# Mixer C's block merges in 64x64 corners, row broadcasts by one transpose, layer 0's modulation tiles in pairs, and eight more modulation sums beside the first FF matrix

## Chip, cores and metric

One Trainium2 chip, one of its cores. The metric is device time in microseconds from the start of the program to its end, as the median of several runs; a profiled execution of the same program gives the trace. TensorE's granted clock has two levels, 1.2 and 2.4 GHz, which the profile gives as 0.50 and 1.00.

## What is computed

Two layers of a backbone with three parallel token mixers and an MLP, for a stream of 128 context tokens and one of 256 latent tokens, all in fp32:

```python
# two layers (DEPTH = 2), residual stream x of 128 context and 256 latent tokens, D_MODEL = 1024, fp32
mod = silu(cond) @ w_ada[l] + b_ada[l]                       # 6 x 1024 per stream: shifts, gains, gates
sh1, sc1, g1, sh2, sc2, g2 = split(mod, 6)
h = rmsnorm(x, norm1_g) * (1 + sc1) + sh1
a, b, c, gates = split(h @ w_in)                              # one input projection, 6576 columns
oa = window_attention(a)                                      # mixer A, 8 heads, sink logits, cached context
ob = latent_attention(b)                                      # mixer B, 8 heads, compressed latents
oc = bidir_gated_delta(c)                                     # mixer C, 4 heads, two directions, chunks
y = sum_j sigmoid(gates_j) * (o_j @ w_branch[j])              # three merges
x = x + g1 * (y @ w_out)
h = rmsnorm(x, norm2_g) * (1 + sc2) + sh2
x = x + g2 * (square(relu(h @ w_ff1)) @ w_ff2)                # D_FF = 4096
# after both layers: final rmsnorm; also returned: keys, values, latents and the final states of C
# inside mixer C, per chunk:  t_mat = inverse(eye + a_mat), a_mat strictly lower triangular
```

## The kernel before

**Layout.** Hidden states stand as 8 tiles of 128 channels by T = 384 tokens. A projection (`project`, L504) takes one weight tile of 128x1024, split by `split` (L146) into two parts `hi` and `lo` on ScalarE and VectorE, and issues 3 x 8 matmuls of 384 columns on TensorE (`mm3`, L150 to L153), into one of three PSUM banks of the pool `pg`. Weights come by `weights` (L131) through three raw buffers `raw` of the pool `wp`, by DMAs on the queue of SyncE (SP). Other PSUM pools are `pc` (two banks, tag c, `bank()`), `pf` (one pair of banks, tag f, `twin()`) and `po` (one bank).

**What sets the order.** All loops are unrolled. A planner puts the instructions of each engine into one fixed order by priority, estimated time and due buffers; each engine then works through its own order and waits on semaphores. `phase` and `stream` (L67, L73) give the priorities: within a phase of a layer what stands in the stream "chain" goes first, "fill" after it. So TensorE's order is a chain (mixer C, then mixer B) with projections of the merges filled in where the planner expects the chain to wait. `tc.issue_after(i)` makes the matmuls traced inside it follow `i` in the order, so that a run of small matmuls stays together.

**Mixer C** (L786 to L973). Per chunk n of 128 tokens (three: one of context, two latent) and direction d (two), a unit triangular system of 128x128 per head (four heads) is inverted: VectorE solves the 32x32 diagonal blocks of all by substitution (L844 to L849), the results are turned (L851, L853), and a loop over n and d (L859 to L899) merges blocks of 32 into 64 and of 64 into 128. In it `bdmask` (L107) spreads the 32x32 results over the block diagonal (L870), `mask5` (L865) takes the blocks beside the diagonal, four products of 128x128x128 per step run over the heads (L876, L884), four of 64 columns (L881), and two steps of four 64x64x64 products (L891, L896) with copies between. f32 products are recorded as two matmuls each. Then the recurrence over chunks follows (`new_values`, `correct`, `write_state`, `outputs`; tiles `g`, 24 buffers), and mixer B in the next phase. `merge(0)` (mixer A's) fills around mixer C, `merge(2)` (C's) around mixer B, `merge(1)` (B's) comes last; a merge is eight blocks of a gate projection and half as many matmuls for the branch (L512 to L535).

**Row broadcasts.** `rstd_rows` (L200) and the end of mixer C (L983 to L986) need a value per token as a row on all partitions. `pieces` (L177) cuts the column into three bf16 parts with four small VectorE steps, `rows` (L188) multiplies each, broadcast, with a bf16 identity: three matmuls per column of 128 tokens. 24 columns per layer: 3 for each of four norms, 12 for mixer C.

**Modulation.** Layer 0's first third is made at the start (`lead`); `ada` (L277) makes the rest beside `merge(2)` and `merge(1)`: each step loads one tile of 128x1024 of `w_ada` (512 KB) and issues four products into four column strips, then yields; `merge` takes `steps` of them per block, (1, 1) beside `merge(2)` from the raw weight buffers, (3, 3) beside `merge(1)` from three buffers `araw`. For layer 1 `ada_sums` (L294) sums 96 tiles of 256 KB on VectorE (L313, two instructions a tile) during layer 0's FF, one tile per block of the first matrix (32 blocks, L1118) and two per quarter row of the second (L1140), and brings each quarter's sums through 8 small products into the strips (L319).

## Time and profile before

| | before |
|---|---|
| median of 3 runs | 1564.96 us (1561.77 to 1565.35) |
| profiled execution | 1564.52 us |
| its span, first to last instruction | 1562.7 us |
| mean granted clock | 0.993 |
| DMA over the span | 134 GB/s read and written, 0.43 of 16 engines |

The span is what the trace covers; the execution's own time has 1.8 us around it. In the rows below, PE is TensorE's matmul row and PEld its weight loads, DVE is VectorE, ACT is ScalarE. Matmuls are pipelined: a row's duration goes from issue to a modelled end, and the next one starts long before that end. L-numbers are lines of the kernel; out<-in gives the program's tile names, then partitions x columns.

### The profile page before, as it was taken

Reading aid. Unit: us, or ns where it says so; the run is one execution under the profiler, and the core shown is the slowest. Engines: PE = TensorE matmul, PEld = TensorE weight load, DVE = VectorE, ACT = ScalarE, POOL = GpSimd, SP = SyncE. Lnnn points to the kernel's source line nnn. Section 1 sums busy time; section 2 is a strip of 40 time slices with the busy share of each in tenths; the row PEclk is TensorE's granted clock in tenths of the full one; section 3 lists DMA queues with packets and bytes.
Section 4 is the critical chain, followed back from the end, with each engine's and each line's share of the span. In section 5 each row is a group of like instructions: output and inputs, shape, how many; then the busy total and the mean of one; then the engine's idle time right before and its main releaser. Section 6 shows DMA issues by size and latency. Waiting matters only on the chain.

```text
span 1562.7 us, 25131 instructions
## 1 busy us (share of the span) xinstructions
PE 1521.6 (97%) x9652; PEld 1396.2 (89%) x9652; DVE 1013.9 (65%) x2187; ACT 771.8 (49%) x1522; POOL 12.9 (1%) x34
## 2 busy tenths in 40 slices
PE   5999999999999999999999999999999999999998
PEld 3898788987888999999988987889888999999997
DVE  4667896475435877789986778955655565553332
ACT  3466633346524666643344676334465446664222
POOL 0000100000000000000000001000000000000000
PEclk9999999999999999999998999999999999999999
DMA  9532131143488555578763331311424434433332
GB/s 315 162 103 88 48 95 48 59 145 105 141 291 279 160 175 176 176 236 259 252 187 98 95 95 47 96 49 58 129 61 135 130 118 126 126 122 129 128 122 81
DMA packets 80857, 212.82 MB, mean 136 GB/s; under 512 B 8801, under 2 KB 24545, under 8 KB 80609
## 3 DMA queue, kind: packets, MB, share of 16 engines
q1 hardware_dynamic: 80736, 211.21, 42.7%
q8 instruction: 76, 1.25, 0.3%
q14 instruction: 45, 0.36, 0.1%
HBM read 204.59 MB, written 4.75 MB: 134 GB/s over the span
## 4 chain that ended last, share of the span: by engine, by line
PE 86%; DVE 8%; DMA 4%; ACT 1%; issue 1%; SPq 0%; DVEq 0%; ACTq 0%
PE g L151 22%; PE g L153 22%; PE g L152 22%; PE c L156 9%; PE f L156 3%; DMA araw<-in_w_ada_dram 2%; PE o L156 2%; PE f L443 2%; DVE wlo L148 2%; PE g L156 1%; DVE h L847 1%; DVE blk L849 1%; DMA mraw<-in_w_ada_dram 1%; PE c L151 1%; PE c L153 1%
## 5 line engine op out<-in xcount | busy, mean ns | idle before, releaser
L147 ACT CAST whi<-raw 128x1024 fp32r<-128x1024 f32 x268 | 280.8, 1048 | 463.6 <-PE g L152 408.0
L153 PE MATMUL g<-hh,wlo 128*128 128x384 f32 (+1 forms) x1440 | 495.2, 345 | 2.8 <-DVE wlo L148 2.7
L151 PE MATMUL g<-hh,whi 128*128 128x384 f32 (+1 forms) x1440 | 494.8, 345 | 3.1 <-ACT hh L229 1.5
L152 PE MATMUL g<-hl,whi 128*128 128x384 f32 (+1 forms) x1440 | 493.6, 344 | 1.3 <-DVE hl L230 1.0
L148 DVE TENSOR_TENSOR wlo<-raw,whi 128x1024 fp32r<-128x1024 f32 x268 | 326.0, 1217 | 168.5 <-PE g L153 123.1
L151 PEld LDWEIGHTS g<-hh,whi 128*128 128x128 f32 x1440 | 272.2, 189 | 14.9 <-issue 6.3
L153 PEld LDWEIGHTS g<-hh,wlo 128*128 128x128 f32 x1440 | 272.5, 189 | 12.4 <-DVE wlo L148 6.0
L152 PEld LDWEIGHTS g<-hl,whi 128*128 128x128 f32 x1440 | 272.2, 189 | 8.1 <-issue 2.7
L151 PE MATMUL g<-fh,whi 128*128 128x384 f32 x512 | 172.9, 338 | 0.0
L152 PE MATMUL g<-fl,whi 128*128 128x384 f32 x512 | 172.1, 336 | 0.0
L153 PE MATMUL g<-fh,wlo 128*128 128x384 f32 x512 | 172.1, 336 | 0.0
L313 DVE SCALAR_TENSOR_TENSOR aacc<-araw,cs,aacc 128x512 f32<-128x512 f32 x168 | 116.5, 747 | 11.0 <-DMA araw<-in_w_ada_dram 6.9
L151 PEld LDWEIGHTS g<-fh,whi 128*128 128x128 f32 x512 | 96.2, 188 | 1.6 <-issue 1.6
L152 PEld LDWEIGHTS g<-fl,whi 128*128 128x128 f32 x512 | 96.3, 188 | 0.0
L153 PEld LDWEIGHTS g<-fh,wlo 128*128 128x128 f32 x512 | 96.3, 188 | 0.0
L156 PE MATMUL c<-g,g 128*128 128x128 f32 (+1 forms) x608 | 77.5, 274 | 3.6 <-DVE g L870 3.1
L156 PEld LDWEIGHTS c<-g,g 128*128 128x128 f32 (+1 forms) x608 | 69.9, 182 | 11.3 <-ACT g L878 4.0
L151 PE MATMUL g<-brh,whi 128*128 128x384 f32 x192 | 66.4, 346 | 0.4 <-ACT whi L147 0.4
L152 PE MATMUL g<-brl,whi 128*128 128x384 f32 x192 | 65.7, 342 | 0.0
L153 PE MATMUL g<-brh,wlo 128*128 128x384 f32 x192 | 65.6, 342 | 0.0
L424 ACT ACTIVATE at_p<-at_p,at_nm 128x384 f32<-128x384 f32 (+1 forms) x96 | 51.8, 541 | 24.7 <-DVE at_nm L421 23.9
L148 DVE TENSOR_TENSOR fl<-fa,fh 128x384 fp32r<-128x384 f32 x64 | 35.6, 556 | 41.9 <-ACT fh L147 41.9
(312 smaller groups left out, 1862.3 us busy)
## 6 DMA issues: line engine op xcount, KB each, us to landing
raw<-in_w_ff_dram SPq DMA_DIRECT2D x128, 512.0 KB, 3.6
raw<-in_w_in_dram SPq DMA_DIRECT2D x102, 512.0 KB, 3.6
araw<-in_w_ada_dram SPq DMA_DIRECT2D x96, 256.0 KB, 3.4
raw<-in_w_branch_dram SPq DMA_DIRECT2D x24, 512.0 KB, 3.6
araw<-in_w_ada_dram SPq DMA_DIRECT2D x24, 512.0 KB, 6.4
raw<-in_w_out_dram SPq DMA_DIRECT2D x16, 512.0 KB, 4.3
mraw<-in_w_ada_dram SPq DMA_DIRECT2D x8, 512.0 KB, 9.2
mraw<-in_w_ada_dram SPq DMA_DIRECT2D x16, 256.0 KB, 7.6
```

What stands on the lines that cost most here:

```text
L147: S.copy(hi, src)
L148: V.tensor_tensor(out=lo, in0=src, in1=hi.bitcast(F32), op=ALU.subtract)
L151: PE.matmul(ps, lhsT=wh, rhs=rh, start=start, stop=False)
L152: PE.matmul(ps, lhsT=wh, rhs=rl, start=False, stop=False)
L153: PE.matmul(ps, lhsT=wl, rhs=rh, start=False, stop=stop)
L156: return PE.matmul(ps, lhsT=lhsT, rhs=rhs, start=start, stop=stop)
L313: V.scalar_tensor_tensor(out=acc[:, s, :], in0=raw, scalar=cs[:, k, s:s + 1], in1=acc[:, s, :], op0=ALU.mult, op1=ALU.add)
L424: S.activation(sm[:, :nk], sm[:, :nk], AF.Exp, bias=nm[:, u:u + 1], scale=-1.0, accum_out=den[:, u:u + 1])
L443: PE.transpose(pt[:, j * P:(j + 1) * P], ps_[half, n][:, c * P:(c + 1) * P], ident)
L847: V.tensor_tensor(out=tmp, in0=Cb[:, j + 1:, j:j + 1].to_broadcast([P, r, w]), in1=X[:, j:j + 1, :w].to_broadcast([P, r, w]), op=ALU.mult)
L849: V.tensor_tensor(out=X[:, j + 1:, :w], in0=X[:, j + 1:, :w], in1=tmp, op=ALU.subtract)
```

## The change

1. **Block merges.** The loop now goes over chunks alone and does both directions in five steps of 64x64x64 products: 16 (both directions, both diagonal corners), 8, 16, 8 and 8. Partners lie in opposite corners of the array: rows 0 to 63 with columns 0 to 63 and rows 64 to 127 with columns 64 to 127 in steps 1 to 3, the two corners off the diagonal in steps 4 and 5, the partners into different banks of `twin()`. `corners` traces the product whose inputs come last first and lets the others follow it. The 32x32 results are spread over 64 columns instead of 128 (`bd2`), into one tile `x0s` that all chunks use, and the result is written back into `Mg`. The copies of a step are split over VectorE and ScalarE, or are four VectorE subtracts of 64x256.
2. **Rows.** `pieces` is no longer called for rows; `rows` is one f32 transpose per column, of the broadcast column.
3. **Layer 0's modulation.** A step is a pair of tiles: both DMAs, then 8 products, the second tile's first. Steps per block are (1, 0) beside `merge(2)` and (1, 2) beside `merge(1)`, there with four `araw` buffers instead of three.
4. **Layer 1's sums.** The 8 small products of a quarter start with the second stream's and follow one another; every fourth block of the first FF matrix takes two tiles, 40 there instead of 32, so the second matrix takes 56 and ends without any.
5. Buffers: `g` 22 instead of 24, `h` 7 instead of 3.

```diff
-    bdmask = cst[:, C_BD:C_BD + P]
+    bd2 = mk(cp, [P, 64], "bd2")
...
-    def rows(b, j0, n):
+    def rows(y, j0, n):
         ps = bank()
         for j in range(n):
-            for i in range(3):
-                mm(ps[:, j * P:(j + 1) * P], b[i][:, j0 + j:j0 + j + 1].to_broadcast([P, P]), ident16, i == 0, i == 2)
+            PE.transpose(ps[:, j * P:(j + 1) * P], y[:, j0 + j:j0 + j + 1].to_broadcast([P, P]), ident)
         return ps[:, :n * P]
...
-        return rows(pieces(rsqrt(ps[:, 0:3], 3, scale)), 0, 3)
+        return rows(rsqrt(ps[:, 0:3], 3, scale), 0, 3)
...
             for k in range(KT):
+                raws = []
                 for half in range(2):
+                    raws.append(mk(ada_pool[0], [P, 1024], ada_pool[1], bufs=ada_pool[2]))
                     c0 = r * 2048 + half * 1024
-                    raw = mk(ada_pool[0], [P, 1024], ada_pool[1], bufs=ada_pool[2])
-                    nc.sync.dma_start(raw, A["w_ada"][l, k * P:(k + 1) * P, c0:c0 + 1024])
-                    rv = raw.rearrange("p (b g i) -> p g b i", b=8, g=4)
+                    nc.sync.dma_start(raws[half], A["w_ada"][l, k * P:(k + 1) * P, c0:c0 + 1024])
+                def block(half, g):
+                    rv = raws[half].rearrange("p (b g i) -> p g b i", b=8, g=4)
+                    return mm(ps[32 * g:32 * g + 32, half * 256:half * 256 + 256].rearrange("p (b i) -> p b i", b=8),
+                              cs[:, k, :], rv[:, g], start=k == 0 and half == 1, stop=k == KT - 1 and half == 0)
+                first = block(1, 0)
+                with tc.issue_after(first.ins):
+                    for g in range(1, 4):
+                        block(1, g)
                     for g in range(4):
-                        mm(ps[32 * g:32 * g + 32, half * 256:half * 256 + 256].rearrange("p (b i) -> p b i", b=8),
-                           cs[:, k, :], rv[:, g], start=k + half == 0, stop=k + half == KT)
-                    if k + half == KT:
-                        modulation(l, r, ps)
-                    yield
+                        block(0, g)
+                if k == KT - 1:
+                    modulation(l, r, ps)
+                yield
...
-                        for s in range(2):
+                        def block(s, g):
                             av = acc[:, s, :].rearrange("p (b g i) -> p g b i", b=4, g=4)
+                            return mm(ps[32 * g:32 * g + 32, q * 128:q * 128 + 128].rearrange("p (b i) -> p b i", b=4),
+                                      pick[:, s, :], av[:, g], start=q == 0 and s == 1, stop=q == 3 and s == 0)
+                        first = block(1, 0)
+                        with tc.issue_after(first.ins):
+                            for g in range(1, 4):
+                                block(1, g)
                             for g in range(4):
-                                mm(ps[32 * g:32 * g + 32, q * 128:q * 128 + 128].rearrange("p (b i) -> p b i", b=4),
-                                   pick[:, s, :], av[:, g], start=q + s == 0, stop=q + s == 4)
+                                block(0, g)
...
+            V.tensor_tensor(out=bd2, in0=cst[:, C_BD:C_BD + 64], in1=cst[:, C_BD + 64:C_BD + P], op=ALU.add)
...
-            return mk(ccp, [P, 4, P], "g", bufs=24)
+            return mk(ccp, [P, 4, P], "g", bufs=22)
...
-            return mk(ccp, [P, 4, 64], "h", bufs=3)
+            return mk(ccp, [P, 4, 64], "h", bufs=7)
...
+        heads = lambda t: t.rearrange("p (h c) -> p h c", h=4)
+        blocks = lambda t: t.rearrange("p h (b c) -> p h b c", b=2)
+        def corners(items, make):
+            first = make(items[-1], 0)
+            with tc.issue_after(first.ins):
+                for h in range(4):
+                    for it in items[::-1]:
+                        if (it, h) != (items[-1], 0):
+                            make(it, h)
+        four = [(d, b) for d in range(2) for b in range(2)]
+        at = lambda d, h: slice(d * 256 + h * 64, d * 256 + h * 64 + 64)
+        side = lambda d: slice(d * 256, d * 256 + 256)
+        x0s = blk().rearrange("p a b -> p (a b)").rearrange("p (i h c) -> p i h c", i=4, h=4)
+        X0, X0T = [x0s[:, 0], x0s[:, 1]], [x0s[:, 2], x0s[:, 3]]
         for n in range(3):
+            M5 = [h4() for _ in range(2)]
             for d in range(2):
                 u0 = (2 * n + d) * 4
+                M = Mg[n, d]
+                for hs in half:
+                    V.tensor_tensor(out=M5[d][hs], in0=M[hs, :, hs],
+                                    in1=mask5[d][hs, hs].unsqueeze(1).to_broadcast([64, 4, 64]), op=ALU.mult)
+                for dst, c in ((X0T[d], (Xc, XcT)[d]), (X0[d], (XcT, Xc)[d])):
+                    V.tensor_tensor(out=blocks(dst), in0=c[:, u0:u0 + 4, :].unsqueeze(2).to_broadcast([P, 4, 2, 32]),
+                                    in1=bd2.rearrange("p (b c) -> p b c", b=2).unsqueeze(1).to_broadcast([P, 4, 2, 32]),
+                                    op=ALU.mult)
+            WT = [h4() for _ in range(2)]
+            ps = twin()
+            corners(four, lambda i, h: mm(ps[i[1]][half[i[1]], at(i[0], h)], M5[i[0]][half[i[1]], h, :], X0T[i[0]][half[i[1]], h, :]))
+            for d in range(2):
+                for b, hs in enumerate(half):
+                    (S.copy if b else V.tensor_copy)(WT[d][hs].rearrange("p h c -> p (h c)"), ps[b][hs, side(d)])
+            X1T = [h4() for _ in range(2)]
+            pt = twin()
+            corners((0, 1), lambda d, h: mm(pt[d][half[d], at(0, h)], X0[d][half[d], h, :], WT[d][half[d], h, :]))
+            for d in range(2):
+                hs = half[d]
+                V.tensor_tensor(out=X1T[d][hs], in0=X0T[d][hs], in1=heads(pt[d][hs, 0:256]), op=ALU.subtract)
+            ps = twin()
+            corners(four, lambda i, h: mm(ps[i[1]][half[i[1]], at(i[0], h)], WT[i[0]][half[i[1]], h, :], X0[i[0]][half[i[1]], h, :]))
+            for d in range(2):
+                for b, hs in enumerate(half):
+                    V.tensor_tensor(out=Mg[n, d][hs, :, hs], in0=X0[d][hs], in1=heads(ps[b][hs, side(d)]), op=ALU.subtract)
+            W2 = [h4() for _ in range(2)]
+            pt = twin()
+            corners((0, 1), lambda d, h: mm(pt[d][half[1 - d], at(0, h)], Mg[n, d][half[d], h, half[1 - d]], X1T[d][half[d], h, :]))
+            for d in range(2):
+                S.copy(W2[d][half[1 - d]].rearrange("p h c -> p (h c)"), pt[d][half[1 - d], 0:256])
+            ps = twin()
+            corners((0, 1), lambda d, h: mm(ps[1 - d][half[d], at(0, h)], W2[d][half[1 - d], h, :], Mg[n, d][half[1 - d], h, half[1 - d]]))
+            for d in range(2):
                 hs, os = half[d], half[1 - d]
-                M = Mg[n, d]
-                M5 = g4()
-                V.tensor_tensor(out=M5, in0=M, in1=mask5[d].unsqueeze(1).to_broadcast([P, 4, P]), op=ALU.mult)
-                M2 = h4()
-                V.tensor_copy(M2[hs], M[hs, :, os])
-                X0, X0T = M, g4()
-                for dst, c in ((X0T, (Xc, XcT)[d]), (X0, (XcT, Xc)[d])):
-                    V.tensor_tensor(out=dst.rearrange("p h (b c) -> p h b c", b=4),
-                                    in0=c[:, u0:u0 + 4, :].unsqueeze(2).to_broadcast([P, 4, 4, 32]),
-                                    in1=bdmask.rearrange("p (b c) -> p b c", b=4).unsqueeze(1).to_broadcast([P, 4, 4, 32]),
-                                    op=ALU.mult)
-                ps = bank()
-                for h in range(4):
-                    mm(ps[:, h * P:(h + 1) * P], M5[:, h, :], X0T[:, h, :])
-                WT = g4()
-                S.copy(flat(WT), ps)
-                pt = bank()
-                for h in range(4):
-                    mm(pt[hs, h * 64:h * 64 + 64], X0[:, h, hs], WT[:, h, hs])
-                ps = bank()
-                for h in range(4):
-                    mm(ps[:, h * P:(h + 1) * P], WT[:, h, :], X0[:, h, :])
-                X1T = h4()
-                V.tensor_tensor(out=X1T[hs], in0=X0T[hs, :, hs], in1=pt[hs, 0:256].rearrange("p (h c) -> p h c", h=4),
-                                op=ALU.subtract)
-                V.tensor_tensor(out=flat(X0), in0=flat(X0), in1=ps, op=ALU.subtract)
-                ps = bank()
-                for h in range(4):
-                    mm(ps[os, h * 64:h * 64 + 64], M2[hs, h, :], X1T[hs, h, :])
-                W2 = h4()
-                S.copy(W2[os].rearrange("p h c -> p (h c)"), ps[os, 0:256])
-                ps = bank()
-                for h in range(4):
-                    mm(ps[hs, h * 64:h * 64 + 64], W2[os, h, :], X0[os, h, os])
-                V.tensor_scalar(out=X0[hs, :, os], in0=ps[hs, 0:256].rearrange("p (h c) -> p h c", h=4), scalar1=-1.0,
-                                scalar2=None, op0=ALU.mult)
-                Xi[n, d] = X0
+                V.tensor_scalar(out=Mg[n, d][hs, :, os], in0=heads(ps[1 - d][hs, 0:256]), scalar1=-1.0, scalar2=None, op0=ALU.mult)
+                Xi[n, d] = Mg[n, d]
...
-        r = pieces(r)
...
-        merge(2, more, (1, 1))
+        merge(2, more, (1, 0))
         es.close()
         ab.close()
         with tc.tile_pool(name=f"ada{l}", bufs=1, reuse_waits="tile") as pool:
-            ada_pool[:] = pool, "araw", 3
-            merge(1, more, (3, 3))
+            ada_pool[:] = pool, "araw", 4
+            merge(1, more, (1, 2))
...
-            next(more, None)
+            for _ in range(2 if t % 4 == 3 else 1):
+                next(more, None)
```

## Rows read from the trace of the kernel before

**Rows 1.** The page: busy us, share of the span and instructions of each engine.

```profile
PE 1521.6 (97%) x9652; PEld 1396.2 (89%) x9652; DVE 1013.9 (65%) x2187; ACT 771.8 (49%) x1522; POOL 12.9 (1%) x34
```

**Rows 2.** Stages: window, length, busy PE, PEld, DVE, ACT, POOL, clock, DMA share, GB/s.

```profile
227.20:264.90 37.70, 36.31 (x303) 30.76 (x303) 30.18 (x46) 9.64 (x17) 0.00 (x0) 1.00 0.14 43
...
302.40:427.00 124.60, 123.26 (x762) 101.25 (x762) 73.08 (x193) 66.75 (x144) 0.00 (x0) 1.00 0.39 124
427.00:492.00 65.00, 63.40 (x478) 54.11 (x477) 29.03 (x45) 19.87 (x28) 0.00 (x0) 1.00 0.86 291
```

**Rows 3.** In order of time, layer 0's first merge of blocks: start, us, what.

```profile
228.23 0.97 PEld L156 LDWEIGHTS c<-g,g 128*128 128x128 f32 x8 [1.89 <-DVE g L870]
228.24 1.16 PE L156 MATMUL c<-g,g 128*128 128x128 f32 x8 [1.57 <-DVE g L870]
...
229.15 0.42 PE L153 MATMUL g<-hh,wlo 128*128 128x384 f32 x1
...
229.43 0.59 ACT L878 COPY g<-c 128x512 f32<-128x512 f32 x1 [5.94 <-PE c L156]
...
230.07 1.77 PE L156 MATMUL c<-g,g 128*64 128x64 f32 x16
230.79 0.41 DVE L886 TENSOR_TENSOR h<-g,c 64x256 f32<-64x256 f32 x1 [0.60 <-PE c L156]
...
231.77 0.54 PEld L156 LDWEIGHTS c<-h,h 64*64 64x64 f32 x8
231.77 0.68 PE L156 MATMUL c<-h,h 64*64 64x64 f32 x8
...
232.37 0.44 PE L151 MATMUL g<-hh,whi 128*128 128x384 f32 x1
...
233.61 0.68 PE L156 MATMUL c<-g,h 64*64 64x64 f32 x8
```

**Rows 4.** The same view, the last merge of blocks in layer 0.

```profile
261.08 1.77 PE L156 MATMUL c<-g,g 128*64 128x64 f32 x16
262.61 0.42 PE L151 MATMUL g<-hh,whi 128*128 128x384 f32 x1
```

**Rows 5.** The same view: row halves in mixer A, column strips of the sums.

```profile
143.14 0.30 PEld L156 LDWEIGHTS f<-kA,qA 64*128 64x128 f32 x4 [0.38 <-issue]
...
804.54 0.65 PE L156 MATMUL g<-aacc,pick 128*32 128x128 f32 x16
805.12 0.38 PE L156 MATMUL c<-cst,sqacc 128*128 128x1 f32 x2
```

**Rows 6.** The same view on ACT, end of layer 0's mixer B.

```profile
422.04 0.48 ACT L1074 COPY br<-o 128x384 f32<-128x384 f32 x1 [0.62 <-PE o L156]
...
429.06 0.49 ACT L523 ACTIVATE gate<-g 128x384 f32<-128x384 f32 x1 [3.00 <-PE g L153]
```

**Rows 7.** The same view on PE: row broadcasts, and transposes of mixer C.

```profile
308.54 0.84 PE L156 MATMUL c<-ident,piece 128*128 128x128 bf16 x12
309.19 0.42 PE L153 MATMUL g<-hh,wlo 128*128 128x384 f32 x1
...
267.28 0.66 PE L925 MATMUL c<-cst,kq 128*128 128x128 f32 x4
267.69 0.42 PE L151 MATMUL g<-hh,whi 128*128 128x384 f32 x1
```

**Rows 8.** Start of layer 1: VectorE in order of time, and one stage.

```profile
809.87 0.17 DVE L182 CAST piece<-rs_y 128x3 bf16<-128x3 f32 x1
...
813.30 0.74 DVE L227 SCALAR_TENSOR_TENSOR tmp<-x,gp,c 128x128 f32<-128x128 f32 x2 [0.79 <-PE c L156]
...
824.00:827.00 3.00, 1.88 (x7) 1.28 (x6) 2.93 (x5) 1.78 (x4) 0.00 (x0) 0.50 0.00 0
```

**Rows 9.** In order of time on PE: one modulation tile of layer 0 beside `merge(2)`.

```profile
320.80 0.64 PE L156 MATMUL g<-raw,cs 128*32 128x256 f32 x8
321.37 0.44 PE L151 MATMUL g<-hh,whi 128*128 128x384 f32 x1
```

**Rows 10.** The second half of layer 0's first FF matrix, and the sums' instruction.

```profile
600.00:668.00 68.00, 68.00 (x411) 67.09 (x410) 54.07 (x93) 46.04 (x83) 0.00 (x0) 1.00 0.57 182
...
L313 DVE SCALAR_TENSOR_TENSOR aacc<-araw,cs,aacc 128x512 f32<-128x512 f32 x168 | 116.5, 747 | 11.0 <-DMA araw<-in_w_ada_dram 6.9 <-ACT aacc L311 4.0
```

## Prediction

> **What bounds the kernel now.** I read the busy shares first: TensorE's matmul row is 1521.6 of 1562.7 us and VectorE's 1013.9 [rows 1]. A busy TensorE may still be waiting, since the modelled ends of its matmuls overlap, so the second view is the busy table cut into the stages that the change touches. In the stage of the block merges TensorE is busy 36.31 of 37.70 us, from the end of mixer C to the end of mixer B 123.26 of 124.60, and in the last merge 63.40 of 65.00 with the DMA engines at 0.86 and 291 GB/s [rows 2]. The third view, the instructions in order of time, says what "busy" is made of. A filler matmul (a gate or a branch projection, 384 columns) starts about every 0.17 us, and between the steps of mixer C's chain the order holds as many of them as fit: 0.92 us of them from 229.15 to 230.07, 1.24 from 232.37 to 233.61 [rows 3]. So TensorE never waits long for the chain, it works on something that has to be done anyway. What counts is therefore **the time from the first instruction of a group to the first of the next (its slot)**, and a slot taken away is a gain as long as filler remains to cover the chain's waits.
>
> **Block merges, work on TensorE.** For one chunk and direction the old slots are: 228.24 to 229.15, 0.91 us (four products 128x128, each recorded as two matmuls); 230.07 to 231.77, 1.70 us (four of 64 columns, then four of 128); 231.77 to 232.37, 0.60 us; and the group at 233.61, which has the shape of the one before, 0.60 us [rows 3]. That is 3.81 us. The last of the six has 261.08 to 262.61, 1.53 us, for the second [rows 4], so 3.65; I take 3.7, and six in a layer are 22.1 us.
>
> The new code has, for a chunk with both directions, two steps of 16 products and three of 8, all 64x64x64. Eight records of that shape, one behind the other in one corner, take a slot of 0.60 us [rows 3]. Whether two opposite corners work at the same time is shown by no row of before. Upper bound, not at all: 32 records are 0.60 + 24 x 0.54/8 = 2.2 us and 16 are 1.14, so 2 x 2.2 + 3 x 1.14 = 7.8 us against 2 x 3.7 = 7.4, a loss of 0.4 us per chunk. Lower bound, two for one: 16 records take 0.60 and 32 take 1.1 (the second half at 0.54, the span of its loads), so 2 x 1.1 + 3 x 0.6 = 4.0 us. The nearest rows are the two kinds of halves that the kernel already has. Mixer A's scores use the upper and the lower 64 rows: their four weight loads of 128 columns span 0.30 us, where eight such loads in a row span 0.97, over 0.11 each, and four would span some 0.5 [rows 3, 5]; so they went two by two. The modulation sums use four column strips, and their 16 records have a slot of 804.54 to 805.12, 0.58 us, or 36 ns each [rows 5], half of the 68 ns of a serial 64x64. An opposite corner differs in rows and in columns from its partner, so I take the lower bound: 22.1 - 3 x 4.0 = 10.1 us per layer, **20.2 us** in both.
>
> The Trainium skill, page "TensorE: Matmul & The Clock Gate", section "Wait — 56ns, not 53.3ns?", says that with hardware decode off a matmul costs the sequencer about 62 ns whatever its size. By that, an estimate from the page, the 112 records of a chunk would be 6.9 us and nearly nothing would be gained. The 36 ns of [rows 5] disagree with it.
>
> **Block merges, the chain.** The new order is strict: the five steps take turns with one pair of PSUM banks, so each waits until the one before is copied out. A step costs its slot, 0.28 us until the copy starts (229.15 to 229.43) and the copies. By the 0.41 us of a 64x256 subtract on VectorE, and between 0.30 (half of the 128x512 copy's 0.59) and the same 0.41 on ScalarE [rows 3], the copies of the five steps are 0.8, 0.8, 1.6, 0.7 and 0.8 us (two, two, four, two and two in one queue). With 4.0 of slots and 5 x 0.33 (the 0.28 and a hand-over back of 0.05, from the copy's end at 230.02 to 230.07) that is 10.4 us per chunk, 31 per layer, against 36.7 us now, from 228.24 [rows 3] to the cut at 264.90 where the recurrence begins [rows 2]. Before the first group three of the new VectorE products of 256 columns must be ready where one of 512 was enough, for which TensorE already waits 1.57 us [rows 3]: three times 0.41 to 0.5 against 0.82 to 0.9, so some 0.6 us more, twice: **+1.2 us**. VectorE is busy 30.18 of 37.70 us in this stage [rows 2]; its work shrinks with the tiles, so it does not become the bound.
>
> **Does filler last?** TensorE's work shrinks by 10.1 us per layer there, the chain by some 4.7 (36.7 to 32, the 0.6 in it); the other 5.4 us must come from filler used earlier. Mixer B's last output was copied at 422.04, and the first gate of the last merge, which needs nothing of mixer B, was read only at 429.06 [rows 6]. Two of its gates can run before that (24 matmuls of some 0.173, 4.15 us each; it has two gate buffers): 8.3 us of spare filler. 5.4 fits, so the gain reaches the end; without that cover it would cost the same 5.4 us per layer.
>
> **Rows by one transpose.** Four columns cost 12 bf16 matmuls now, slot 308.54 to 309.19, 0.65 us or 0.163 a column; four f32 transposes of the same size have 267.28 to 267.69, 0.41 us or 0.103 a column [rows 7]. There are 24 columns per layer, so 48 x 0.06 = **2.9 us**. Four small VectorE steps go with each use. They matter where TensorE starves: at the start of layer 1. There the reciprocal root was ready when the first of the pieces started at 809.87, and the modulation that reads the row began at 813.30, after a wait for TensorE [rows 8]. Without the pieces three transposes (0.3 us) and a hand-over stand between, so it begins near 810.7, 2.6 us earlier. TensorE's stretch of starving, which ends in a granted clock of 0.50 (1.2 GHz) at 824 to 827 [rows 8], should shift by as much: **2.5 us**, bounds 0 (another queued wait takes its place) and 8 (the clock stays at 2.4 GHz: a filler needs twice its 0.17 us there). At the other uses I count the transposes alone.
>
> **Layer 0's modulation in pairs.** A single tile's eight records have a slot of 320.80 to 321.37, 0.57 us; 16 records together cost about 1.0 by the 0.054 us of a 256-column record in four strips (0.43 of the 0.57 for eight, the rest paid once) [rows 9]. In the middle merge eight singles become four pairs of about 1.0 us: 4.6 - 4.0, and four interruptions of the filler less at 0.1: **1.0 us**. In the last merge the work is the same and the DMA engines run at 291 GB/s [rows 2], so I take nothing; bounds: 4 us gained (no waits left, eight times 0.4 and the same again in weights) and 6 lost, because in every second block four tiles are issued ahead of the weights on SP's queue instead of three, 0.5 MB or 1.8 us at 291 GB/s, four times, less what the weight buffers cover. In the middle merge a pair holds two of the three raw weight buffers; the weights' loads then queue on SP behind one buffer. That merge has room (its 8 blocks of 36 matmuls are some 50 us of filler for mixer B's 124.6), bound 0 to 5 us lost.
>
> **Sums beside the first FF matrix.** Eight more of them there are 8 x 2 x 0.747 us = 12 us on VectorE, which is busy 54.07 of 68 us in its second half [rows 10]; over its 768 matmuls of some 0.18 us, 138 us, this adds 0.09, so 0.88 at most. Nothing, bound 2 us lost. Their end moves away from the start of layer 1, where the last 16 records stood at 804.54 [rows 5]: worth 0 to 0.7, taken at nothing.
>
> **The sum.** The profiled execution took 1564.52 us, the median of the runs is 1564.96, so one stands for the other. 1564.5 - 20.2 + 1.2 - 2.9 - 2.5 - 1.0 = **1539.1 us**.
>
> **Rivals.**
> Corners one after the other: the upper bound above. Instead of 20.2 gained, 6 x 0.4 = 2.4 lost: 1539.1 + 22.6 = 1561.7 us. For it: no row shows two corners at once. Against: rows and columns each do it [rows 5].
> Filler runs short: if the merge stage lasts L us per layer instead of 32, the missing 5.4 + (L - 32) exceeds 8.3 from L = 34.9 on, and each further us idles TensorE in mixer B. With L = 36.7, no shorter than now, 1539.1 + 2 x 1.8 = 1542.7; with L = 42, 1553. For it: 15 waits in a strict row, with weight splits of 1.2 us in the same VectorE queue. Against: the old chain had 18 waits.
> The strict row becomes the bound (the slower side): the same mechanism with L over 50.2 (16.7 us per chunk, 3.3 per step instead of 2.1) passes 1569.7; L = 52 gives 1573 us. A starved TensorE also falls to 1.2 GHz, as at 824 us [rows 8], and then needs twice as long for every chain group, which is what could drive it there.
> Layer 1 starts without the drop of the clock: 5.5 us more, 1533.6.
>
> **How the numbers follow.** Forecast 0.68, with a range of its own of 1533 to 1545 from the bounds of the modulation and the start of layer 1. Better start 0.06; filler short 0.14; corners in series 0.07; strict row 0.05. The range to hold the time 8 times in 10 takes the forecast, the better start and most of the short filler: 1529 to 1552. About 0.3% (4.7 us) can be told from no change. Faster by more holds the forecast, the better start and the short filler, 0.88; the serial corners end within it, 0.07; slower 0.05.
>
> **What would show it.** Groups of 16 and 32 records of 64x64 with slots of 0.6 and 1.1 us confirm the corners, 1.1 and 2.2 refute them. Five groups per chunk with fillers between, and the last merge's first gate read before mixer B's last output, confirm the filler. At the start of layer 1 the modulation should follow the reciprocal root within 0.9 us instead of 3.4. I am wrong if matmul gaps open in mixer B, if ScalarE waits for raw weights in the middle merge, or if the last merge takes longer than its 65.00 us.

## The result, and the profile after

The changed kernel takes 1543.91 us as the median of four runs (1543.46 to 1544.19), the kernel before 1563.53 beside it: a ratio of 0.9874, 95% interval 0.9857 to 0.9891. The forecast was 1539.1. The medians are 19.6 us apart, where the sum had 25.4. The profiled executions, from which all stages below are read, took 1543.46 us against 1564.52, 21.1 less. The busy line answers [rows 1]: TensorE's busy time shrank by 25 us, VectorE's by 10.

```profile
PE 1496.4 (97%) x9748; PEld 1380.7 (90%) x9748; DVE 1004.4 (65%) x2172; ACT 768.9 (50%) x1522; POOL 12.9 (1%) x34
```

**The corners.** In order of time on TensorE, the first groups of layer 0 (start, duration, what; answers [rows 3]). The slot of a group runs to the line under it:

```profile
226.84 1.35 PE L156 MATMUL f<-blk,h 64*64 64x64 f32 x32 [2.61 <-DVE blk L903]
228.12 0.69 PE L151 MATMUL g<-hh,whi 128*128 128x384 f32 x1
232.49 0.68 PE L156 MATMUL f<-h,blk 64*64 64x64 f32 x16
233.10 0.45 PE L152 MATMUL g<-hl,whi 128*128 128x384 f32 x1
234.35 1.15 PE L156 MATMUL f<-blk,h 64*64 64x64 f32 x32
235.43 0.44 PE L152 MATMUL g<-hl,whi 128*128 128x384 f32 x1
237.55 0.68 PE L156 MATMUL f<-h,g 64*64 64x64 f32 x16
238.16 0.44 PE L153 MATMUL g<-hh,wlo 128*128 128x384 f32 x1
```

32 records take 1.08 us, 16 take 0.61: the lower bounds of the prediction, 1.1 and 0.60. The first group waits 2.61 us where 1.57 was the wait before [rows 3]; its slot is 1.28 us. VectorE's order from the last turn of the solved blocks to that group shows the chain:

```profile
223.15 1.21 DVE L869 STREAM_TRANSPOSE blk<-blk 128x1024 f32<-128x1024 f32 x1
224.28 0.38 DVE L900 TENSOR_TENSOR h<-g,cst 64x256 f32<-64x256 f32 x1
224.58 1.08 DVE L903 TENSOR_TENSOR blk<-blk,bd 128x256 f32<-128x256 f32 x2
225.68 0.42 DVE L900 TENSOR_TENSOR h<-g,cst 64x256 f32<-64x256 f32 x1
226.11 1.09 DVE L903 TENSOR_TENSOR blk<-blk,bd 128x256 f32<-128x256 f32 x2
```

X0 of direction 0, which the first group does not read, stands ahead of X0T of direction 1, which it does. And the clock falls, as these windows say (columns as in [rows 2]; the clock is the third number from the end):

```profile
226.84:227.63 0.79, 0.79 (x27) 0.79 (x29) 0.79 (x3) 0.00 (x0) 0.00 (x0) 1.00 0.00 0
227.63:231.04 3.41, 3.41 (x22) 3.06 (x18) 2.94 (x5) 0.73 (x2) 0.00 (x0) 0.50 0.38 88
231.04:265.00 33.96, 33.30 (x419) 28.84 (x417) 23.22 (x51) 13.75 (x36) 0.00 (x0) 1.00 0.23 71
```

The 16 fillers behind the first group take 4.37 us in layer 0 and 4.10 in layer 1, where sixteen at 0.174 are 2.8. Before, the clock did not fall there in either layer.

**The chain.** The merges of a layer take longer than before, not shorter. From the first group of a chunk to the first group of the next it is 14.9 and 13.5 us, and 12.1 from the third chunk's first group to the end of its last: 40.6 us in layer 0 and 40.5 in layer 1, where the prediction had 31 and the kernel before 36.7. But products of the recurrence (`c<-g,g` of 128 columns) now run between the steps, from 241.11 on; before, they began behind all merges, at 264.9. TensorE in order of time:

```profile
241.11 0.71 PE L156 MATMUL c<-g,g 128*128 128x128 f32 x4
241.76 1.15 PE L156 MATMUL f<-blk,h 64*64 64x64 f32 x32
...
255.28 1.15 PE L156 MATMUL f<-blk,h 64*64 64x64 f32 x32 [0.29 <-DVE g L932]
...
266.79 0.68 PE L156 MATMUL f<-g,h 64*64 64x64 f32 x16
```

From the end of the merges to the last group of the recurrence it is then 23.6 us instead of 36.6, and from the first group of the merges to mixer B's last output 179.5 instead of 193.8.

**Filler.** It was not short, though not by the sign that was named. ScalarE's rows around the end of layer 0's mixer B, answering [rows 6]: its last output is copied at 406.37, and the eight gates of the last merge are read from 416.84 on, still behind it. The gate at 411.35 is the last one of `merge(2)`, which before was read ahead of mixer B's end, at 420.94 against 422.04. So with mixer B over, a block of the middle merge was left to do.

```profile
406.37 0.48 ACT L1107 COPY br<-o 128x384 f32<-128x384 f32 x1 [3.84 <-PE o L156]
411.35 0.48 ACT L538 ACTIVATE gate<-g 128x384 f32<-128x384 f32 x1
416.84 0.49 ACT L538 ACTIVATE gate<-g 128x384 f32<-128x384 f32 x1 [1.38 <-PE g L153]
```

From the row broadcasts to the end of mixer B TensorE's listed waits are 1.5 us together, 1.2 before. Those of ScalarE for raw weights, which the prediction named as a sign, are 4.4 us in three waits, the longest 2.6, where they were 2.8 in four, the longest 1.0.

**Rows and pairs.** On TensorE in order of time: eight row transposes have a slot of 0.81 us, four 0.38, so 0.10 a column (the price taken from [rows 7]); a pair of tiles in the last merge, 16 records, 1.00 us, two pairs 1.86.

```profile
295.96 1.06 PE L192 MATMUL c<-cst,rs_y 128*128 128x128 f32 x8
296.77 0.42 PE L151 MATMUL g<-hh,whi 128*128 128x384 f32 x1
297.38 0.63 PE L192 MATMUL c<-cst,rs_y 128*128 128x128 f32 x4
297.76 0.42 PE L151 MATMUL g<-hh,whi 128*128 128x384 f32 x1
...
434.66 1.07 PE L156 MATMUL g<-araw,cs 128*32 128x256 f32 x16
435.66 0.45 PE L151 MATMUL g<-hh,whi 128*128 128x384 f32 x1
442.16 1.93 PE L156 MATMUL g<-araw,cs 128*32 128x256 f32 x32
444.02 0.44 PE L151 MATMUL g<-hh,whi 128*128 128x384 f32 x1
```

In the last merge of before, TensorE's list of waits (who waits for whom: us in total, times, longest) has one entry, and after it has none:

```profile
PE g L156 <- DMA araw<-in_w_ada_dram: 1.5, 3, 0.5
```

**Start of layer 1.** The modulation now starts 0.64 us after the reciprocal root is ready, at 797.37, and 5.7 us behind the last residual; before it was 8.65 ([rows 8], 813.30, the residual at 804.65). But the 3 us do not reach the end. Two projections of layer 1 start before the row is known, on x without it (the early sums, later in the tiles `kab` and `sqacc`); each holds a PSUM bank until it is copied out. TensorE in order of time: the early sums end, two projection products run, and then it stands.

```profile
801.40 0.34 PE L153 MATMUL g<-hh,wlo 128*128 128x386 f32 x1
801.58 0.34 PE L151 MATMUL g<-hh,whi 128*128 128x384 f32 x1
801.76 0.34 PE L152 MATMUL g<-hl,whi 128*128 128x384 f32 x1
808.59 1.06 PE L151 MATMUL g<-hh,whi 128*128 128x384 f32 x2 [6.49 <-ACT kab L499]
```

The releaser is the copy of the first early sum out of PSUM. ScalarE's order has it behind all of the modulation:

```profile
807.35 0.82 ACT L228 ACTIVATE hh<-tmp,mod 128x128 fp32r<-128x128 f32 x2 [0.89 <-DVE tmp L226]
808.08 0.46 ACT L499 COPY kab<-g 48x384 f32<-48x384 f32 x1
808.44 0.47 ACT L499 COPY sqacc<-g 128x384 f32<-128x384 f32 x1
```

The clock is at 0.50 from 804.48 to 814.72, as long as the fall that began at 823.2 before.

**A stage that nothing was predicted for.** The 768 products of layer 1's second FF matrix run without a gap in both kernels, and take 133.28 us before and 135.84 after. From start to start (the pitch) that is 173.3 and 176.7 ns. Windows of 120 us, first of before, then of after (the number of products stands behind busy PE):

```profile
1425.00:1545.00 120.00, 120.00 (x694) 120.00 (x694) 42.91 (x49) 33.00 (x36) 0.00 (x0) 1.00 0.35 116
```

```profile
1400.00:1520.00 120.00, 120.00 (x681) 120.00 (x681) 41.66 (x48) 32.99 (x36) 0.00 (x0) 1.00 0.37 119
```

### The profile page after: what moved, and what is told of

Read it like the earlier page. It is cut to its first block, busy times and chain, and to the rows that moved or that the text cites. A ratio compares the mean times of both kernels' runs of the same rounds, so it can differ in the third digit from the quotient of the medians.

```text
span 1541.7 us, 25278 instructions
## 1 busy us (share of the span) xinstructions
PE 1496.4 (97%) x9748; PEld 1380.7 (90%) x9748; DVE 1004.4 (65%) x2172; ACT 768.9 (50%) x1522; POOL 12.9 (1%) x34
## 4 chain that ended last, share of the span: by engine, by line
PE 85%; DVE 9%; DMA 3%; ACT 2%; issue 1%; SPq 0%; DVEq 0%; ACTq 0%
PE g L151 22%; PE g L153 22%; PE g L152 22%; PE c L156 5%; PE f L156 4%; PE o L156 2%; PE f L458 2%; DVE wlo L148 2%; PE g L156 1%; DMA mraw<-in_w_ada_dram 1%; DVE blk L865 1%; DVE h L863 1%; DMA araw<-in_w_ada_dram 1%; PE c L151 1%; PE c L153 1%
## 5 line engine op out<-in xcount | busy, mean ns | idle before, releaser
L350 DVE SCALAR_TENSOR_TENSOR x<-g,mod,x 128x128 f32<-128x128 f32 x64 | 23.7, 412 | 54.2 <-PE g L153 51.1
L1158 ACT ACTIVATE fa<-fa,fb 128x128 f32<-128x128 f32 (+1 forms) x128 | 51.1, 446 | 0.7 <-DVE fa L1156 0.7
```

The lines of the kernel that those rows point to most:

```text
L350: V.scalar_tensor_tensor(out=x[k][:, c], in0=ps[:, c], scalar=m[:, b0 + k, s:s + 1], in1=x[k][:, c], op0=ALU.mult, op1=ALU.add)
L1158: S.activation(a[:, c], a[:, c], AF.Relu, bias=b[:, s:s + 1])
```

## The experiments

Twelve kernels ran. Stages are cut at the same instructions in all: the start of the last turn of mixer C's solved blocks (223.15 above), the last tile of y on ScalarE, the first and last product of the second FF matrix. In us, from the trace of each kernel's profiled execution:

| stage | before | after | merges alone | rows alone | pairs alone | one step | addresses + one step |
|---|---|---|---|---|---|---|---|
| layer 0 to the merges of blocks | 226.1 | 223.2 | 222.4 | 225.9 | 225.8 | 223.0 | 223.3 |
| from there to y | 264.3 | 253.1 | 257.3 | 262.7 | 262.3 | 252.9 | 253.0 |
| w_out and first FF matrix | 175.3 | 176.6 | 175.8 | 177.8 | 176.1 | 176.2 | 175.4 |
| second FF matrix | 138.9 | 138.8 | 139.1 | 139.9 | 139.1 | 139.7 | 139.1 |
| layer 1 to the merges of blocks | 200.2 | 199.8 | 199.3 | 193.9 | 193.2 | 191.5 | 193.0 |
| from there to y | 243.4 | 234.2 | 236.5 | 241.3 | 243.2 | 234.4 | 234.4 |
| w_out and first FF matrix | 169.0 | 168.6 | 169.0 | 168.6 | 169.0 | 168.6 | 168.6 |
| second FF matrix | 133.3 | 135.8 | 133.3 | 133.3 | 133.3 | 135.8 | 133.3 |
| to the end | 12.3 | 11.7 | 11.7 | 12.2 | 12.2 | 12.2 | 12.2 |
| span | 1562.7 | 1541.7 | 1544.3 | 1555.6 | 1554.2 | 1534.4 | 1532.4 |
| median of the runs | 1563.5 | 1543.9 | 1545.9 | 1553.9 | 1556.0 | 1536.9 | 1534.8 |

The median of before was 1562.8 to 1563.5 beside each set. A column is one execution. The runs of the rows alone go from 1550.3 to 1557.6 us and those of the pairs alone from 1552.1 to 1559.9, so a difference of 2 or 3 us that stands in one column only may be that execution's.

### Neighbours in the same corner

```diff
-                for h in range(4):
-                    for it in items[::-1]:
+                for it in items[::-1]:
+                    for h in range(4):
```

> The changed kernel with the order of the products within a group turned: all four heads of one corner, then of the next, so that neighbours in TensorE's order share a corner. Same products, same count. Theory A (two opposite corners run at once): a group of 32 records goes from 1.08 to 1.8 to 2.2 us and one of 16 from 0.61 to 1.0 to 1.2; per chunk 2 x 0.9 + 3 x 0.5 = 3.3 us, six chunks 20 us if all of it lies on TensorE's path: 1555 to 1566 us. Theory B (64-row records simply are short, or the issue of them sets the pitch): the groups stay at 1.1 and 0.6 us and the time at 1543.9.

Measured: 1554.49 us, 10.6 more; ratio to before 0.9949 (0.9934 to 0.9964). In order of time, of this kernel:

```profile
237.13 1.54 PE L156 MATMUL f<-blk,h 64*64 64x64 f32 x32
238.59 0.45 PE L152 MATMUL g<-hl,whi 128*128 128x384 f32 x1
240.72 0.96 PE L156 MATMUL f<-h,g 64*64 64x64 f32 x16
241.61 0.44 PE L153 MATMUL g<-hh,wlo 128*128 128x384 f32 x1
```

1.46 us for 32 and 0.89 for 16: longer, though less than theory A's figures, and the time ends just below its range. The starts of the single records say why: neighbours of one corner come 58 ns apart, a record of the other corner 4 to 6 ns after its partner, and where the order goes from one corner to the next a few still pair up. In the changed kernel every partner comes 6 to 8 ns after the other. Without the few pairs that are left the loss would be larger. Per chunk 2 x 0.38 + 3 x 0.28 = 1.6 us, six chunks 9.6; the two merge stages are 9.2 longer. So opposite corners do run at once, and what a group costs goes to the end almost in full. The Trainium skill, page "TensorEngine Tiling (Array Packing)", section "Key Properties", says that different tiles of the array load and multiply in parallel; these groups agree, with 1.08 us for 32 records partner by partner and 1.46 corner by corner.

### The block merges alone

```diff
-            return mk(ccp, [P, 4, P], "g", bufs=24)
+            return mk(ccp, [P, 4, P], "g", bufs=22)
...
+        bd2 = mk(ccp, [P, 64], "bd2")
...
-        for n in range(3):
-            for d in range(2):
+        for n in range(3):
+            M5 = [h4() for _ in range(2)]
+            for d in range(2):
...
```

The loop over the block merges is that of the change, line for line.

> The kernel before with the block merges of the change alone (the doubled mask in mixer C's own pool, so that all the tiles of the FF matrices keep their addresses). Theory A (the steps of the prediction, with what the comparison of the two traces added): corners -20.2, first wait +1.2 as predicted or +2.1 idle and +3.2 of half clock as the changed kernel showed: 1543 to 1546 us against 1563.3 (-17 to -20). Theory B (a good part of the 20 us in the changed kernel came from the rows and the pairs, and the merges give less): above 1548 us. The second FF matrix of layer 1 keeps its pitch of 173.33 ns.

Measured: 1545.86 us, 17.0 less; ratio 0.9893 (0.9876 to 0.9910). From the merges to y it is 7.1 us shorter in layer 0 and 7.0 in layer 1, 14.0 in all; ahead of the first group the same waits, 2.62 and 2.60 us, and the same falls of the clock. The other 3.6 us of the trace lie ahead of the merges, where the clock stands at 0.50 for 3.4 us against 10.2 before; nothing shows that the edit does this. So the time lies in theory A's range, but the merges themselves are worth 14.0 us of the 17.0.

### The rows alone, the pairs alone

The first is the diff's second part alone, with spare bytes where the pieces lay; the second its third and fourth part, steps and buffers included.

```diff
+    mk(sp, [P, 96], "pad", bufs=1)
...
-            for i in range(3):
-                mm(ps[:, j * P:(j + 1) * P], b[i][:, j0 + j:j0 + j + 1].to_broadcast([P, P]), ident16, i == 0, i == 2)
+            PE.transpose(ps[:, j * P:(j + 1) * P], y[:, j0 + j:j0 + j + 1].to_broadcast([P, P]), ident)
...
```

> The kernel before with the rows by one transpose alone (three transposes of fp32 in place of nine products of bf16 pieces, no pieces), 384 spare bytes in the pool of small tiles in place of those of the pieces. Theory A (the prediction): rows -2.9 and layer 1's start -2.5, 1563.3 - 5.4 = 1557.9 us. Theory B (as the changed kernel's trace reads: the modulation is early, but TensorE then stands at the two early sums' PSUM banks for 6.5 us, and the start gives back all but 0.9): 1559 to 1561 us, with one long wait for the copy of the early sums in layer 1 only.

> The kernel before with the modulation products in pairs alone (both halves of a block of w_ada at once, four buffers, the merges' steps and the FF steps as in the change). Theory A (the prediction): middle merge -1.0, last merge 0, FF sums 0: 1562.3 us. Theory B (as the changed kernel's trace reads: the last merge lost its waits for the transfers, 0.44 to 0.53 us in every second block, some 1.5 us): 1560.5 to 1561.5 us. Theory C (the pairs cost in the FF stage what they give in the merges): 1563 us or more.

Measured: rows 1553.91 us (ratio 0.9939, 0.9922 to 0.9956), pairs 1556.03 (0.9959, 0.9943 to 0.9974): 9.0 and 6.9 less, both more than any theory gave. The three parts add up to 32.9 us, the whole change gave 19.6. The table shows where. From the merges to y the parts do add: 7.1 + 1.6 + 2.0 = 10.7 in layer 0, where the whole change has 11.3, and 7.0 + 2.1 + 0.2 = 9.3 in layer 1, where it has 9.2. But from layer 1's start to its merges the rows alone save 6.2 us and the pairs alone 7.0, the whole change 0.4. ScalarE's order in the kernel with the rows alone:

```profile
813.33 0.47 ACT L484 COPY kab<-g 48x384 f32<-48x384 f32 x1
814.15 1.75 ACT L229 ACTIVATE hh<-tmp,mod 128x128 fp32r<-128x128 f32 x4 [0.35 <-DVE tmp L227]
816.95 1.05 ACT L148 CAST whi<-raw 128x1024 fp32r<-128x1024 f32 x1 [1.04 <-PE g L153]
817.91 1.48 ACT L229 ACTIVATE hh<-tmp,mod 128x128 fp32r<-128x128 f32 x4
819.30 0.45 ACT L484 COPY sqacc<-g 128x384 f32<-128x384 f32 x1
```

Here the planner put one copy ahead of the modulation and one into it, so two PSUM banks are free when the modulated tiles arrive, and in TensorE's order two projections take each tile in turn: 6 products a tile, 1.0 us, near the 1.3 us in which tiles come (in the kernel before, the first of eight starts at 813.30 and the last at 822.60). Before and after, they follow one another, 3 products a tile; before has the second copy behind all of the modulation, at 826.87, the changed kernel both. Nothing in either part touches the copies or the projections; the planner's order there depends on what surrounds it. The pairs alone have the same order, and in both the clock does not fall while the modulation runs.

### The early sums copied out sooner

```diff
-            hh, hl = modulated(rb, gp1, mod0, 0)
+            hh, hl, got = [], [], []
             for i, ps in enumerate(pss):
...
+                S.copy(t, ps[:, :T])
                 V.tensor_copy(b, ps[:, T:])
-                S.copy(t, ps[:, :T])
+                got.append((M, t, b))
+                his, los = modulated(rb, gp1, mod0, 0, range(4 * i, 4 * i + 4))
...
```

> The changed kernel with ScalarE's copies of layer 1's two early sums out of PSUM put ahead of the halves of the modulation, not behind all of it. Theory A (the 6.49 us in which TensorE stands at layer 1's start are the two PSUM banks that these copies hold): the stretch falls to under 3 us, since the first projections can then follow hh as it comes, the fall of the clock behind it goes or shrinks, and the time falls by 2 to 6 us, to 1538 to 1542 us. Theory B (the projections would wait for the modulated tiles anyway): the idle time comes back as waits for hh and hl, and the time stays within 1 us of 1543.9.

Measured: 1543.21 us, 0.7 less than the changed kernel, within what runs differ by. Theory B, in another form: the wait of 6.49 us is gone and one of 5.17 stands in its place, for the transposes of kab, which the planner has put behind six products while kab's last step stays behind the modulation.

```profile
803.21 0.34 PE L152 MATMUL g<-hl,whi 128*128 128x384 f32 x1
808.72 0.84 PE L597 MATMUL c<-cst,kab 48*128 48x48 f32 x3 [5.17 <-ACT kab L507]
```

### One step per tile again

```diff
-            for _ in range(2 if t % 4 == 3 else 1):
+            for _ in range(1):
```

> The changed kernel with one step of layer 1's sums per tile of the first FF matrix, as before, in place of 40 in 32 tiles: the last part of the change undone. The instruction order that comes of it differs at layer 1's start: the first two projections take the modulated tiles in turn (20 changes between them in the first 48 products, 5 in the changed kernel), the two early sums' copies stand ahead of and within the modulation, and the transposes of kab stand behind 50 products, as in the kernels with the rows alone and the pairs alone. Theory A (the order at layer 1's start is what the two single parts gained beyond the prediction): the 6.5 us wait and the fall of the clock behind it vanish, -5 to -7 us, 1537 to 1539 us. Theory B (the steps in the FF stage have the price of the prediction, nothing, and the order at the start is worth nothing): 1543.9 us.

Measured: 1536.85 us, 7.1 less than the changed kernel; ratio to before 0.9835 (0.9820 to 0.9850). Theory A. Layer 1's start takes 191.5 us instead of 199.8, the clock does not fall while the modulation runs, and the waits of TensorE there are short (line, waited for, us in total, times, longest):

```profile
PE g L151 <- ACT sqacc L499: 0.6, 1, 0.6
PE c L592 <- ACT kab L502: 0.6, 1, 0.6
PE g L151 <- ACT hh L228: 0.3, 1, 0.3
```

The FF stage itself hardly moves: 176.6 to 176.2 and 138.8 to 139.7. So the steps cost nothing where they were priced and 7 us where they were not: they changed an order that runs 140 us later. Of the 8.3 us of this stage some 1.5 are another fall of the clock, 3.4 us from 954.67 on in the changed kernel, which this execution lacks; the kernel with addresses and one step, which has it, is 6.8 us shorter there. And the steps alone do not make the slow order: the pairs alone have the same 40 steps and the fast one.

### The wait ahead of the merges

```diff
-                for dst, c in ((X0T[d], (Xc, XcT)[d]), (X0[d], (XcT, Xc)[d])):
+            for x0, cc_ in ((X0T, (Xc, XcT)), (X0, (XcT, Xc))):
+                for d in range(2):
+                    u0 = (2 * n + d) * 4
...
```

> The changed kernel with VectorE's order ahead of the block merges turned: both M5, then X0T of both directions, and X0 (which the first group of products does not read) last. Theory A (the wait ahead of the first group is VectorE's chain, and the clock falls because of its length): TensorE's idle time there goes from 2.61 to about 1.57 us (one multiplication of 1.08 us less), the clock no longer falls in the 16 fillers behind it (4.4 and 4.1 us back to 2.8), and each layer gains 1.0 + 1.3 to 3.2 us: 1537 to 1540 us. Theory B (the clock falls there whatever the wait): only the 1.0 us per layer, 1541.8 us. Theory C (something else releases the first group): no change, 1543.9.

Measured: 1544.99 us (1543.00 to 1548.13), not to be told from the changed kernel. The wait is 2.14 and 2.11 us instead of 2.61, some 0.5 less, half of what was expected: the turn takes one multiplication out of the chain, and the 1.08 us of the expectation are the row of two, 0.54 each. The clock fell all the same, and in layer 0 for longer:

```profile
229.20:236.00 6.80, 6.45 (x30) 5.44 (x30) 3.16 (x5) 0.73 (x2) 0.00 (x0) 0.50 0.51 153
```

So this turn does not settle what makes the clock fall there. In a later kernel the same turn has M5 of the first chunk on GpSimd.

### Where the tiles lie

In the first kernel the doubled mask moves to the pool of small tiles with 128 spare bytes, so that weights and FF tiles lie at their addresses of before; in the second without the spare bytes, so that only the weights and the modulated x do.

```diff
-    bd2 = mk(cp, [P, 64], "bd2")
+    bd2 = mk(sp, [P, 96], "bd2", bufs=1)[:, 0:64]
```

> The changed kernel with the 256 bytes of the doubled mask taken from the pool of small tiles, with 128 spare bytes behind it: weights, modulated x and the squared FF tiles lie at the byte addresses that they had before. Theory A (addresses): the pitch of the 384-column products of layer 1's second FF matrix goes from 176.67 back to 173.33 ns, 768 x 3.33 ns = 2.6 us, and the time from 1543.9 to about 1541.3 us. Theory B (not the addresses: something that differs from one execution or program to the next): the pitch is 176.67 or 173.33 by chance, and the other kernels of this set show both values at one layout. If it stays at 176.67, the addresses are out.

> The changed kernel with the doubled mask in the pool of small tiles without the spare bytes: weights and modulated x lie where they lay before, the squared FF tiles and x stay where the changed kernel has them, 128 bytes lower than before. Theory A (the address of the streamed FF tiles sets the pitch): 176.67 ns in layer 1's second FF matrix, 1543.9 us. Theory B (the address of the weights sets it): 173.33 ns, 1541.3 us.

Measured: 1542.70 us (1541.03 to 1544.87) and 1544.14 (1543.86 to 1545.18). The runs overlap, the traces do not. First the old addresses, then the kernel in which only the weights went back:

```profile
1400.00:1520.00 120.00, 120.00 (x695) 120.00 (x694) 42.22 (x50) 32.99 (x36) 0.00 (x0) 1.00 0.35 119
```

```profile
1400.00:1520.00 120.00, 120.00 (x681) 120.00 (x680) 42.33 (x49) 33.34 (x37) 0.00 (x0) 1.00 0.35 119
```

The stage takes 133.28 and 135.84 us. Over all fourteen traces it is 133.28 or 133.3 with the FF tiles at the old addresses (before, and seven experiments) and 135.84 with them 128 bytes lower (after, and five), with no exception. So the pitch follows a place, not chance, and not the weights' place; x and other tiles of that side moved by the same 128 bytes, and were not told apart. Layer 0's second FF matrix, with its tiles at the same addresses, keeps 173.3 ns in both; why is open.

### Three edits, and the fastest kernels

Old addresses, the turn with M5 on GpSimd, and kab finished ahead of the modulation:

```diff
+                if i == 0:
+                    V.tensor_tensor(out=t, in0=t, in1=rb[:M], op=ALU.mult)
...
-                    V.tensor_tensor(out=M5[d][hs], in0=M[hs, :, hs],
+                    (V if n else G).tensor_tensor(out=M5[d][hs], in0=M[hs, :, hs],
```

> The changed kernel with three edits at once: the tiles at their addresses of before; ahead of the merges M5 of the first chunk on GpSimd, then X0T of both directions, then X0; at layer 1's start the first early sum is copied out, scaled and shifted before the modulation, the second copied out after half of it. Theory A (each of the three holds): pitch -2.6 us; the wait ahead of the first group 2.6 to about 1.3 us and no fall of the clock behind it, -2 to -5 us in both layers together; layer 1's start, where the early copies alone only moved the wait to the 5.2 us in which TensorE stood for kab, -2 to -5 us: 1531 to 1537 us. Theory B (the waits move once more, to hh at the start and to VectorE's evictions at the merges): 1539 to 1541 us, the pitch alone.

Measured: 1537.43 us (1533.95 to 1538.81), 6.5 less than the changed kernel, 0.4 above theory A's range. The pitch is back (133.28), layer 1's start is 2.3 us shorter, with TensorE waiting piecewise for hh and hl and the clock at 0.50 for 6.8 us; from the merges to y 3.1 and 1.0 less. The turn cost something too: to the merges of layer 0 this kernel takes 3.8 us longer. A weight split of VectorE slipped into the chain, and the two waits ahead of the first group are 0.99 and 1.96 us. While GpSimd worked on M5, 4.17 us from 217.45 on, VectorE's two steps of 128x135 took 0.83 and 0.78 us, in the changed kernel 0.29 and 0.30. And the clock stood at 0.50 for 10.2 us in this stage, not 6.8.

Then old addresses with one step, without and with that turn:

> The changed kernel with the tiles at their addresses of before and one step per tile of the first FF matrix. Theory A (both hold and add): 1543.9 - 2.6 - 5 to 7 = 1534 to 1536 us, and 173.33 ns per product in layer 1's second FF matrix. Theory B (they don't add, since the clock falls elsewhere when TensorE has less to wait for): 1538 us or more.

> The kernel with the old addresses and one step, and with the order ahead of the merges turned as well (M5 of the first chunk on GpSimd, X0T of both directions before X0). Theory A (the wait ahead of the first group is worth what it was in the kernel with the three edits, where the clock no longer fell in layer 0): 1 to 3 us less than the kernel without the turn, 1531 to 1534 us. Theory B (VectorE's split of a weight block slips into the chain ahead of the merges, as it did there, and the turn gains nothing): the same as without it.

Measured: 1534.84 us (1534.36 to 1535.99), ratio to before 0.9819 (0.9804 to 0.9834), and 1534.61 (1533.80 to 1535.93), 0.9817 (0.9803 to 0.9832). Addresses and order at layer 1's start add: 9.1 us less than the changed kernel, theory A of the first. The turn adds nothing: from the merges to y it saves 2.8 and 1.5 us, and as much is lost elsewhere. That is theory B's time, but its reason covers only part: 0.9 us are lost ahead of layer 0's merges and 0.6 ahead of layer 1's, 2.7 in layer 0's projections and FF matrices, which the turn does not touch. Both are faster than the changed kernel.

## Why the prediction was right, and where its steps were off

The direction, the mechanism of the corners and the order of the size were right: 19.6 us of the 25.4 came by the medians, 21.1 in the traces. The account of the chain was wrong, and the forecast held by an overlap that it did not foresee. By the steps:

- **Work of the corners: right.** 1.08 and 0.61 us for 1.1 and 0.60. The choice of the lower bound, from row halves and column strips [rows 5], is what the whole forecast stood on, and the order with neighbours in one corner shows what the other end would have cost.
- **Chain: wrong.** The five steps were to take 10.4 us a chunk and 31 a layer, 32 with the longer wait. They took 40.6 and 40.5, the recurrence's products between them included; what they take without these is not shown. By the prediction's own rival of short filler that would have cost 5.4 + 8.6 - 8.3 = 5.7 us per layer, and the time would have been some 1550 us. It did not come to that, because the recurrence of the first chunk runs between the steps and what follows the merges is 13 us shorter. No step looks at this overlap, and why the planner makes it now and not before was not followed up. Here the forecast was lucky.
- **Filler: right in the result, not in its sign.** From the first group to mixer B's end the chain became 14.3 us shorter in layer 0, more than the 10.1 by which TensorE's work on the merges shrank, so nothing had to come from a supply of filler. No gate of the last merge went ahead of mixer B's end, and a block of the middle merge was left over. Of the signs for being wrong small ones showed: a wait of 1.0 us for a reciprocal root in mixer B's stage, and ScalarE's waits for raw weights, 1.6 us longer together. The last merge, from its first gate to y, took 59.4 us against 61.4 before.
- **The wait ahead of the first group: the term that failed most.** Put at +1.2 us for both layers, measured 2 x 1.04 us of idle time and, behind it, 16 fillers 1.6 and 1.3 us longer and a first group 0.2 and 0.4 longer at 1.2 GHz: some 5.6. Two things were missed. Five VectorE steps, 2.4 us, stand between the turn and the group, not three of 0.41 to 0.5: two halves of M5 came to lie there as well as X0 of direction 0, and one multiplication is 0.54. And a drop of the clock was priced for a starved chain only, not for this wait. With it, merges and wait together gave 14.0 us instead of 19.0; 20.2 - 5.6 would be 14.6.
- **Rows: undersized at the merges, open elsewhere.** The forecast had 2.9 us in all. The kernel with the rows alone gained 3.8 in the two merge stages, and 0.4 in layer 1's first FF matrix, but its layer 0's projections and FF matrices were longer by 3.5 us in that one execution, which was not followed up.
- **Layer 1's start: the size failed, the bound held.** 2.5 us were forecast, 0.4 came, at the end that the prediction had as "another queued wait takes its place". Its sign, the modulation within 0.9 us, was there; what was late next was not the modulation but the PSUM bank behind two copies, which stood in the same ScalarE queue. The other end, 8 us, was just as real: against before, the rows alone came to 6.2, the pairs alone to 7.0 and one step to 8.6.
- **Pairs: 1.0 forecast for the middle merge and nothing for the last, 2.0 measured** for the pairs alone. The bounds of loss did not come: the three waits for transfers of the last merge, 1.5 us, are gone, which is the gain that the forecast put at nothing.
- **Sums beside the FF matrix: nothing where they were priced, but with the other parts 7 us through the order at layer 1's start.** No step of the prediction looks at what a moved instruction does to the planner's order elsewhere.
- **Not foreseen:** 2.6 us lost through 128 bytes in the place of tiles whose use no edit changes; 2.9 us gained ahead of the merges in layer 0, where the clock was at 0.50 for 6.8 instead of 10.2 us, worth 1.7 of them. No run shows that the edit caused this gain; it may be luck of the execution.

## What to carry to other kernels

Products of 64x64 on opposite corners run two at a time if neighbours in the order are partners, so trace them partner by partner. With a planner, or any order written once, compare the order at every place that starves before and after an edit, not only where the edit is: a copy that frees a PSUM bank can stand behind long work in the same queue, and moving it alone may only uncover the next wait (0.7 us here, where the whole order was worth 7). And time the parts alone: their sum, larger than the whole, is what showed that 7 us lay elsewhere.

## What was not expected of the hardware

- Products of 384 columns, each with its own weight load, ran at 173.3 or 176.7 ns from start to start depending on where the tiles of one pool lie: 128 bytes made 2.6 us in 133. Layer 0's same products did not show it.
- The granted clock fell to 1.2 GHz behind a wait of 2.1 to 2.6 us ahead of the corners, in both layers of all nine kernels that had it, while a wait of 1.57 us at the same place left it at 2.4 in both layers of three (before, the rows alone, the pairs alone). With 0.99 and 1.96 us, some 3 us apart, it stayed in layer 0 and fell in layer 1. What decides is open.
- A record of 64x64 in the opposite corner starts 4 to 8 ns after its partner, one of the same corner right behind another 58 ns after.
